# Time mixing in five slots per pair of heads, with two inverses and two last parts at work at once

## The chip, the cores and the metric

The kernel runs on one core of one Trainium2 chip. Its time is the device time in microseconds from start to end of one execution; the kernel before takes 2623.82 us (median of three runs, 2618.25 to 2625.08). All data and products are float32. Large products are done in a faster form, float32r, with each operand split into a rounded part and the rest (H and L in the code); small products are plain float32, and each of these shows up as two instructions in the trace.

## The reference: what is computed

A trunk of two layers on 256 tokens with 2048 channels. Layer 0 does RWKV-7 time mixing, layer 1 banded attention on one shared key and value; each is followed by a squared-ReLU MLP, and every part is scaled and shifted by vectors that are projected from a condition vector `c` (the "ada" products). The change touches time mixing only. With 32 heads of 64 channels it is

```
r, k, v = xr @ w_r, xk @ w_k, xv @ w_v
kk = normalised per head (k * k_k);  k = k * (1 + (a - 1) * k_a)
for t in range(256):                      # per head, S is 64 x 64
    sa = S @ (-kk_t)
    S  = S * w_t + outer(sa, kk_t * a_t) + outer(v_t, k_t)
    y_t = S @ r_t
y = group_norm(y) + (sum over the head of r * k * r_k) * v
out = (y * g) @ w_o
```

## The kernel before

**The chunked form.** The recurrence over 256 tokens is cut into four chunks of 64. Inside a chunk it becomes products of 64x64 matrices and the inverse of one unit triangular 64x64 matrix per chunk and head. Two heads share the 128 partitions, so the loop runs over 16 pairs of heads. Each pair passes through four stages, written as Python generators that give up control (`yield`) after each step:

- The dense stage, `proj_steps`: the two projections k and r of the pair, 2 x 16 steps. A step is one product with 512 columns (line 418) and one with 256 (line 419). It also loads the next weights (512 KB each, ring of six buffers `raw`) and splits them into H on ScalarE (line 384) and L on VectorE (line 387).
- `early`, 9 steps: decay, normalisation and the scaled factors `kr` and `bkh`, the centred values `G`, and the product of the bonus term. VectorE, ScalarE and GpSimd do most of it.
- `invert`, 11 steps: `both(pg, kr)` (line 105) makes the chunk's matrices, a masked copy of which is `X` (line 233). The inverse is then built by doubling from blocks of 2 to blocks of 64: levels 1 to 4 have a first step (`tiles`, line 112, then an addition on VectorE, line 253) and a second (`tiles`, then a transposed copy on VectorE, line 238, and a plain copy on ScalarE, line 269). The last level (lines 255 to 273) has two steps, read out by ScalarE. All results of this chain stand in one buffer of PSUM, `iv`.
- `late`, 10 steps: the chain over the four chunks. For each chunk it makes the right-hand side with the state `zs` (lines 294 and 297), copies it to `G` (299), then the next state (314, 317 or 319) and the outputs `py` (302, 322); behind it group norm, the bonus and the gate (330 to 339).

**The order of the work.** A period of the loop (lines 856 to 883) has in flight `late` of pair p-3, `invert` of p-2, `early` of p-1 and the dense stage of p. It has 11 slots; in each slot every generator advances by its share of steps, first the small ones, then the dense one. From this program order a planner fixes the order on each engine by a model of the durations: an instruction that is ready sooner may go ahead of an older one. `tc.issue_after` puts instructions behind a given one on their engine; here it holds the dense steps behind the small products of the slot before. The small products are not held. The program adds the waits between engines. After 16 pairs come three more periods that drain the pipeline; parts of the next product (`w_o`, `out_steps`, 44 steps) fill them, and `out_proj` does the rest.

**Other work in the loop.** In periods from 2 on, `ada` loads 512 KB of another weight per step into the same ring `raw` and adds it up on VectorE (line 448), five per period, 27 in the drain. Each half of such a vector ends in 32 small products (`ada_sum`, line 460), spread over slots by `fin(2)`.

Of the kernel before, what the change touches and what calls it, by code (L numbers as in the profile page):

```python
# [2 lines left out]

# [14 lines left out]
P = 128  # L18
# [58 lines left out]
class Pair:  # L77
# [3 lines left out]
    EARLY = 9  # L81
# [16 lines left out]
    def both(self, o, rhs):  # L98

        for c in range(4):  # L100
            for half in range(2):
                for i, K, S in self.heads:
                    n = i ^ half
                    nc = self.b.nc
                    nc.tensor.matmul(o[i][C * n:C * n + C, c, :], self.bkh[K, c, i + n, :], rhs[K, c, :],  # L105
                                     start=True, stop=True, tile_position=(C * i, C * n))

    def tiles(self, o, lhsT, rhs, pairs):

        for c in range(4):  # L110
            for R, K in pairs:
                self.b.nc.tensor.matmul(o[QS[K], c, :], lhsT[QS[R], c, :], rhs[QS[R], c, :], start=True, stop=True,  # L112
# [14 lines left out]
    def head_sums(self, ps, parts):  # L127
        for i, t in enumerate(parts):
            self.b.nc.tensor.matmul(ps, self.b.bones, t, start=(i == 0), stop=(i == 1))

    def early(self):
        b, nc, j, k, r, v, s, ch = self.b, self.b.nc, self.j, self.k, self.r, self.v, self.s, self.ch
        pw, vec, cst, e01 = b.pw, b.vec, b.cst, self.e01
        lw = pw.tile([96, 2, P], F32, tag="lw", bufs=2, name="lw")
        nc.sync.dma_start(out=lw, in_=b.d["lora2"][j, :96, 0:2])
        self.lg = pw.tile([P, 2, P], F32, tag="lg", bufs=2, name="lg")
        nc.sync.dma_start(out=self.lg, in_=b.d["lora2"][j, :, 2:4])
        z = b.psm()
        nc.tensor.matmul(z[:, 0:T], lw[:, 0, :], self.tw, start=True, stop=True)
        nc.tensor.matmul(z[:, T:2 * T], lw[:, 1, :], self.ta, start=True, stop=True)  # L140
# [8 lines left out]
        for o in (sw, a):  # L149
# [12 lines left out]
        self.pc = pw.tile([P, 4, 1], F32, tag="pc", bufs=3, name="pc")  # L162
# [11 lines left out]
        self.dg = pw.tile([P, 4, C], F32, tag="dg", bufs=1, name="dg")  # L174
        nc.gpsimd.tensor_tensor(out=self.dg, in0=cst("eye").unsqueeze(1).to_broadcast([P, 4, C]),
                                in1=self.pc.to_broadcast([P, 4, C]), op=ALU.mult)
# [7 lines left out]
        kr = self.kr = self.big("kr", 3)  # L184
        nc.vector.tensor_tensor(out=kr[:, :, 0:C], in0=ch(kk), in1=e0, op=ALU.mult)
        bkh = self.bkh = pw.tile([P, 4, 3, C], F32, tag="bkh", bufs=1, name="bkh")
# [3 lines left out]
        rkp = s()  # L190
        nc.vector.scalar_tensor_tensor(out=rkp, in0=r, scalar=vec("r_k", j), in1=km, op0=ALU.mult, op1=ALU.mult)
        nc.vector.tensor_tensor(out=bkh[:, :, 0, :], in0=ch(km), in1=ch(e2), op=ALU.mult)
        nc.scalar.copy(bkh[C:P, :, 2, :], bkh[C:P, :, 0, :])
        rkp = self.parts(AF.Copy, rkp)
        yield


        G = self.G = pw.tile([P, 2, 4, C], F32, tag="G", bufs=2, name="G")
        pt = b.psm().rearrange("p (a c k) -> p a c k", a=2, c=4)[:, 0]
        for c in range(4):  # L200
            for i, K, S in self.heads:
                nc.tensor.matmul(pt[K, c, :], ch(v)[K, c, :], cst("cen")[K], start=True, stop=True)
        for i, K, S in self.heads:
            nc.scalar.copy(G[K, i], pt[K])
        yield
        pbn = b.psm()[:, :T]
        self.head_sums(pbn, rkp)
        nc.vector.tensor_tensor(out=v, in0=pbn, in1=v, op=ALU.mult)
        yield

    def invert(self):
        b, nc, s, ch, kr = self.b, self.b.nc, self.s, self.ch, self.kr
        cst, pp = b.cst, b.pp

        def every(name):
            return cst(name).unsqueeze(1).to_broadcast([P, 4, H])

        def half(name, bufs):
            return b.pw.tile([P, 4, H], F32, tag=name, bufs=bufs, name=name)


        ui = cst("ui").unsqueeze(1).to_broadcast([P, 4, P])
        X = self.X = b.pw.tile([P, 2, 4, 3, C], F32, tag="X", bufs=2, name="X")
        pg = [pp.tile([P, 4, P], F32, tag="gr", bufs=1, name="gr"),
              pp.tile([P, 16, H], F32, tag="iv", bufs=1, name="iv").rearrange("p (c a) h -> p c (a h)", c=4)]
        self.both(pg, kr)
# [975 lines left out]
```

## Time and profile before

| | before |
|---|---|
| median of three runs | 2623.82 us |
| the profiled execution | 2621.53 us, span 2619.7 us, granted clock 0.994 |
| TensorE busy (products) | 2572.8 us, 98% |
| VectorE / ScalarE / GpSimd busy | 76% / 55% / 8% |
| pair loop: first `r` complete to last `r` complete | 198.4 to 584.5 us |
| drain of the pairs | 584.5 to 661 us |

PE is TensorE, PEld its weight loads, which overlap its products and show the order and pace of its instructions; DVE is VectorE, ACT ScalarE, POOL GpSimd. Busy time of PE is that of pipelined products with modelled ends, so in stretches of small products the starts of the weight loads tell more than the busy share. A mark such as [0.25 <-ACT u L269] on a row is the idle time of the engine before it and what ended it. Line numbers are those of the kernel before.

### The profile page before, as it was taken

How to read it: one execution, taken by the hardware profiler on the slowest of the kernel's cores; microseconds unless marked ns; L12 is line 12 of the kernel's file. 1: busy time of each engine (PE TensorE's matmuls, PEld its weight loads, DVE VectorE, ACT ScalarE, POOL GpSimd, SP SyncE). 2: the span in 40 equal slices, each digit the busy share in tenths (PEclk: the TensorE clock that was granted, in tenths of full speed). 3: DMA queues.
4: the chain of work that ended last, by engine and by line, in shares of the span. 5: the costliest groups of instructions: out<-in, count | busy, mean ns of one | idle time of the engine just before them, and what ended most of it. 6: DMA issues, size and time to landing. Idle time of an engine off the chain costs nothing.

```text
span 2619.7 us, 59049 instructions
## 1 busy us (share of the span) xinstructions
PE 2572.8 (98%) x24138; PEld 2232.6 (85%) x24138; DVE 1988.8 (76%) x2756; ACT 1452.8 (55%) x2709; POOL 207.2 (8%) x366
## 2 busy tenths in 40 slices
PE   7999999999999999999999999999999999999998
PEld 6997777778898888888888998778998888888887
DVE  5678888888778988888888887776779655555554
ACT  3456767674575633466544664676566533566443
POOL 0004333332100000000000000000000000000010
PEclk9999999999999999999999999999999999999999
DMA  9965666557858999999989788866559655555553
GB/s 360 356 239 184 190 189 193 186 181 255 288 182 304 344 367 360 353 332 335 330 313 330 260 302 286 277 233 207 183 193 338 227 188 187 191 186 188 190 188 125
DMA packets 192671, 662.74 MB, mean 253 GB/s; under 512 B 21392, under 2 KB 36112, under 8 KB 192400
## 3 DMA queue, kind: packets, MB, share of 16 engines
q1 hardware_dynamic: 191536, 657.71, 72.3%
q8 instruction: 189, 3.10, 0.5%
q10 hardware_dynamic: 864, 1.26, 0.1%
q14 instruction: 82, 0.67, 0.1%
HBM read 656.79 MB, written 2.10 MB: 252 GB/s over the span
## 4 chain that ended last, share of the span: by engine, by line
PE 90%; DVE 4%; DMA 3%; ACT 2%; issue 1%; POOL 1%; SPq 0%; DVEq 0%; ACTq 0%; POOLq 0%
PE pj L418 44%; PE pj L419 22%; PE pj L408 2%; PE pj L409 2%; PE pj L407 2%; PE iv L112 2%; DVE wL L387 1%; PE m L664 1%; DMA rawa<-w_ada 1%; DMA rawt<-w_ada 1%; PE gr L105 1%; POOL s L171 1%; PE v L767 1%; PE l L757 1%; PE po L1101 1%
## 5 line engine op out<-in xcount | busy, mean ns | idle before, releaser
L418 PE MATMUL pj<-aHL,wH 128*128 128x512 f32 x4128 | 1486.4, 401 | 0.0
L387 DVE TENSOR_TENSOR wL<-raw,wH 128x1024 fp32r<-128x1024 f32 x772 | 936.0, 1218 | 348.8 <-ACT wH L384 344.2
L384 ACT CAST wH<-raw 128x1024 fp32r<-128x1024 f32 x772 | 802.6, 1044 | 684.5 <-PE pj L418 567.0
L419 PE MATMUL pj<-aHL,wL 128*128 128x256 f32 x4128 | 1161.3, 281 | 1.2 <-DVE wL L387 1.1
L418 PEld LDWEIGHTS pj<-aHL,wH 128*128 128x128 f32 x4128 | 779.0, 189 | 185.2 <-issue 7.2
L419 PEld LDWEIGHTS pj<-aHL,wL 128*128 128x128 f32 x4128 | 780.4, 189 | 7.1 <-DVE wL L387 4.9
L418 PE MATMUL pj<-hHL,wH 128*128 128x512 f32 x992 | 348.1, 395 | 0.0
L448 DVE SCALAR_TENSOR_TENSOR acc<-rawm,ct,acc 128x1024 f32<-128x1024 f32 x217 | 279.9, 1290 | 2.6 <-DMA rawm<-w_ada 0.3
L419 PE MATMUL pj<-hHL,wL 128*128 128x256 f32 x992 | 275.5, 278 | 0.0
L418 PEld LDWEIGHTS pj<-hHL,wH 128*128 128x128 f32 x992 | 186.1, 188 | 43.2
L419 PEld LDWEIGHTS pj<-hHL,wL 128*128 128x128 f32 x992 | 186.4, 188 | 0.0
L409 PE MATMUL pj<-aHL,wL 128*128 128x258 f32 (+1 forms) x608 | 171.3, 282 | 1.6 <-DVE wL L387 1.6
L408 PE MATMUL pj<-aHL,wH 128*128 128x258 f32 (+1 forms) x608 | 172.6, 284 | 0.0
L407 PE MATMUL pj<-aHL,wH 128*128 128x258 f32 (+1 forms) x608 | 172.1, 283 | 0.0
L515 POOL TENSOR_TENSOR ss<-ss,scr 128x256 f32<-128x256 f32 x42 | 38.7, 922 | 1586.5 <-ACT scr L511 1586.3
L448 DVE SCALAR_TENSOR_TENSOR acc<-raw,ct,acc 128x1024 f32<-128x1024 f32 x90 | 120.2, 1336 | 0.1
L409 PEld LDWEIGHTS pj<-aHL,wL 128*128 128x128 f32 x608 | 116.0, 191 | 2.2 <-DVE wL L387 2.2
L408 PEld LDWEIGHTS pj<-aHL,wH 128*128 128x128 f32 x608 | 115.0, 189 | 0.1
L407 PEld LDWEIGHTS pj<-aHL,wH 128*128 128x128 f32 x608 | 114.4, 188 | 0.2
L984 DVE SCALAR_TENSOR_TENSOR x<-pj,mod,x 128x256 f32<-128x256 f32 x126 | 60.8, 483 | 55.7 <-PE pj L419 47.1
L948 ACT ACTIVATE t<-t 128x256 f32<-128x256 f32 x104 | 43.4, 418 | 89.7 <-DVE t L947 89.7
L448 DVE SCALAR_TENSOR_TENSOR acc<-rawt,ct,acc 128x1024 f32<-128x1024 f32 x53 | 67.8, 1280 | 16.2 <-DMA rawt<-w_ada 15.9
(268 smaller groups left out, 2981.6 us busy)
## 6 DMA issues: line engine op xcount, KB each, us to landing
raw<-w_up SPq DMA_DIRECT2D x256, 512.0 KB, 4.9
raw<-w_down SPq DMA_DIRECT2D x256, 512.0 KB, 4.6
rawm<-w_ada SPq DMA_DIRECT2D x166, 512.0 KB, 7.0
raw<-w_ada SPq DMA_DIRECT2D x97, 512.0 KB, 3.7
rawa<-w_ada SPq DMA_DIRECT2D x64, 512.0 KB, 8.1
rawm<-w_ada_kv SPq DMA_DIRECT2D x64, 512.0 KB, 6.6
rawt<-w_ada SPq DMA_DIRECT2D x57, 512.0 KB, 6.2
raw<-w_k SPq DMA_DIRECT2D x32, 512.0 KB, 4.2
```

Source lines behind the costliest of these rows:

```text
L112: self.b.nc.tensor.matmul(o[QS[K], c, :], lhsT[QS[R], c, :], rhs[QS[R], c, :], start=True, stop=True, tile_position=(H * R, H * K))
L384: nc.scalar.copy(Hf, raw)
L387: eng.tensor_tensor(out=Lf, in0=raw, in1=Hf, op=ALU.subtract)
L407: nc.tensor.matmul(ps, H[:, i, :], a(kt)[:, 0, :], start=(first and kt == 0), stop=False)
L408: nc.tensor.matmul(ps, H[:, i, :], a(kt)[:, 1, :], start=False, stop=False)
L409: ins = nc.tensor.matmul(ps, L[:, i, :], a(kt)[:, 0, :], start=False, stop=(last and kt == KT - 1))
L418: nc.tensor.matmul(ps, H[:, i, :], a(kt), start=(first and kt == 0), stop=False)
L419: ins = nc.tensor.matmul(ps[:, 0, :], L[:, i, :], a(kt)[:, 0, :], start=False, stop=(last and kt == KT - 1))
L448: nc.vector.scalar_tensor_tensor(out=acc, in0=raw, scalar=ck, in1=acc, op0=ALU.mult, op1=ALU.add)
L515: (eng or nc.gpsimd).tensor_tensor(out=self.ss, in0=self.ss, in1=sq, op=ALU.add)
L948: nc.scalar.activation(t, t, AF.Relu)
L984: nc.vector.scalar_tensor_tensor(out=x, in0=ps[:, i, :], scalar=self.mods[(layer, 5)][:, n:n + 1], in1=x, op0=ALU.mult, op1=ALU.add)
```

## The change

Seven things are changed together, all in time mixing and its drain.

1. Slots per period go from 11 to 5. `invert` (now 10 steps) and `late` (10 steps) each last two periods, so that in each slot the pipeline holds two inverses and two last parts, five generators in all with `early` (8 steps). There are 21 periods instead of 19. `ORDER` fixes which generator goes first in a slot: the older inverse, the younger one, then the others.
2. Every small product of the loop is put behind the TensorE instruction before it (`mm`, with `pinned`), and the dense steps behind the last small product: TensorE's order is the program order.
3. The matrix to be inverted comes from 16 products of its own at the end of `early` (`pd`, then one copy `near`). `both(pg, kr)`, `X`, `G` and `both(pt, dg)` move from `early` and `invert` to `late`.
4. The chain over chunks: the right-hand sides without state are made for all four chunks at once (`pa`), `M` (for the inner two chunks the matrix that takes a state to the next) is made ahead with the help of `kT`, then `state` makes three states `Z`, one per step, and one step each makes all right-hand sides and all outputs.
5. The buffers in PSUM: `iv` becomes one tile of four blocks that are used in turn, `chn` one tile of two blocks; `py` also holds the bonus product.
6. The ring `raw` falls from 6 to 3 buffers in the loop. Outside of it every second load goes to a second ring of 3 (`wx`). More buffers for `kr`, `bkh`, `u` and others.
7. The sums of the ada vectors are done in one go at slot 3 (`fin(HK)`). In the drain 40 steps of `w_o` run instead of 44; the rest follows in `out_proj`. Weights are split at steps 5 and 11 instead of 6 and 15.

```diff
-    EARLY = 9
+    EARLY, INV, LATE = 8, 10, 10
...
+        pd = self.chain()
         for c in range(4):
+            for q in range(4):
+                i = 1 - q // 2
+                K, h = self.heads[i][1], H * (q % 2)
+                b.mm(pd[QS[q], c, :], bkh[K, c, 1, h:h + H], kr[K, c, h:h + C], start=True, stop=True,
+                                 tile_position=(C * i, H * q))
+        near = pw.tile([P, 4, C], F32, tag="da", bufs=2, name="da")
+        nc.scalar.copy(near, pd)
+        da, u = near[:, :, 0:H], self.half("u", 5)
...
     def invert(self):
...
-            pi = pp.tile([P, 16, H], F32, tag="iv", bufs=1, name="iv")[:, 0:4, :]
+            pi = self.block()
...
     def late(self):
...
+        pg = [self.wide(), b.psm().rearrange("p (c k) -> p c k", c=4)]
+        self.both(pg, kr)
...
+        bn = self.parts(AF.Copy, self.rkp)
+        yield
+        pa = self.chain()
+        for c in range(4):
+            for i, K, S in heads:
+                b.mm(pa[S, c, :], X[K, i, c, 0, :], G[K, i, c, :], start=True, stop=True)
+        for i, K, S in heads:
+            nc.scalar.copy(G[S, i], pa[S])
+        pt = self.pair_of_banks()
+        self.both(pt, dg)
+        for c in (1, 2):
+            for i, K, S in heads:
+                b.mm(pt[i][S, 3 + c, :], kr[K, c, 0:C], cst("eye")[K], start=True, stop=True)
...
+        yield
+        pr = self.pair_of_banks()
+        for n in range(4):
+            for m in range(2):
+                for i, K, S in heads:
+                    O = S if m == 0 else K
+                    b.mm(pr[m][O, n, :], u[S, n, :], X[S, i, n, 1 + m, :], start=True, stop=True,
+                                     tile_position=(S.start, O.start))
...
+        def state(c, ps):
+            if c:
+                for i, K, S in heads:
+                    b.mm(ps[K, 0, :], M[K, c - 1, :], Z[K, c - 1, :], start=True, stop=False)
+            for i, K, S in heads:
+                b.mm(ps[K, 0, :], X[:, i, c, 2, :], G[:, i, c, :], start=c == 0, stop=True)
+            nc.scalar.copy(Z[:, c, :], ps[:, 0, :])
+
+        ps = self.chain()
+        for c in (1, 2):
+            for i, K, S in heads:
+                b.mm(ps[K, c, :], kT[S, c - 1, :], X[S, i, c, 2, :], start=True, stop=True)
+        state(0, ps)
+        nc.vector.tensor_tensor(out=M, in0=ps[:, 1:3, :], in1=dg[:, 1:3, :], op=ALU.add)
+        yield
+        state(1, self.chain())
+        yield
+        state(2, self.chain())
+        yield
+        pa = self.chain()
+        for c in (1, 2, 3):
+            for i, K, S in heads:
+                b.mm(pa[S, c, :], X[K, i, c, 0, :], G[K, i, c, :], start=c == 1, stop=False)
+        for c in (1, 2, 3):
+            for i, K, S in heads:
+                b.mm(pa[S, c, :], kr[K, c, 0:C], Z[K, c - 1, :], start=False, stop=c == 3)
+        for i, K, S in heads:
+            nc.scalar.copy(G[S, i, 1:4], pa[S, 1:4])
+        yield
...
-    RAW_BUFS = 6
+    RAW_BUFS = 3
...
-    SLOTS = 11
+    SLOTS = 5
+    _INV = (("invert", 1), ("invert", 0))
+    ORDER = ((*_INV, ("late", 1), ("late", 0), ("early", 0)),) * 3 + ((*_INV, ("early", 0), ("late", 0), ("late", 1)),) * 2
+    DRAIN_STEPS = (10, 7, 7, 8, 8)
...
+    def raw_ring(self):
+        self.nraw += 1
+        if self.wx is not None and self.nraw % 2:
+            return self.wx, "rawx", self.RAW_BUFS
+        return self.wp, "raw", self.RAW_BUFS
...
+    def mm(self, *args, **kw):
+        with self.tc.issue_after(self.last_pe()) if self.pinned else nullcontext():
+            self.nc.tensor.matmul(*args, **kw)
...
+            iv = pi.tile([P, 4, 4, C // 2], F32, name="iv")
+            chn = pp.tile([P, 2, 4, C], F32, name="chn")
+            self.blocks = cycle(iv[:, i] for i in range(4))
+            self.chains = cycle(chn[:, i] for i in range(2))
...
-                        if kt in (6, 15) and src is not None:
+                        if kt in (5, 11) and src is not None:
...
-            stages = ((Pair.late, 10), (Pair.invert, 11), (Pair.early, Pair.EARLY), (None, 2 * KT))
+            stages = ((Pair.late, Pair.LATE, 2), (Pair.invert, Pair.INV, 2), (Pair.early, Pair.EARLY, 1),
+                      (None, 2 * KT, 1))
...
+                    order = sorted(live, key=lambda g: self.ORDER[slot].index(g[3]))
+                    for gens in (order, [dense]):
+                        with nullcontext() if gens is order else tc.issue_after(self.last_pe()):
+                            for g in gens:
                                 while g[2] * self.SLOTS < g[1] * (slot + 1):
                                     next(g[0], None)
                                     g[2] += 1
```

More of the change, by code (lines that the diff above doesn't have):

```diff
@@ L2 @@
 from contextlib import ExitStack, nullcontext
+from itertools import cycle
 import numpy as np
@@ L128, in head_sums @@
         for i, t in enumerate(parts):
[L129 removed]
+            self.b.mm(ps, self.b.bones, t, start=(i == 0), stop=(i == 1))
     def early(self):
@@ L211, in invert @@
-    def invert(self):
[L212 to L226, printed above, removed]
-        da, u = half("da", 2), half("u", 3)
-        for i, K in enumerate(QS):
-            n = H * (i % 2)
-            nc.scalar.copy(da[K], pg[1 - i // 2][K, :, n:n + H])
-        nc.gpsimd.tensor_tensor(out=u, in0=da, in1=every("lev0"), op=ALU.mult)
-        for i in (1, 0):
-            nc.vector.tensor_tensor(out=X[:, i, :, 0:2, :].rearrange("p c a t -> p c (a t)"), in0=pg[i], in1=ui,
-                                    op=ALU.mult)
-        def turned(src):
-            t = half("tt", 1)
-            nc.vector.transpose(out=t.rearrange("p c t -> p (c t)"), in_=src.rearrange("p c t -> p (c t)"))
-            return t
-        nc.vector.tensor_tensor(out=u, in0=u, in1=every("eye_h"), op=ALU.add)
-        tt_ = turned(u)
-        yield
@@ new lines, in early, with half, every, turned @@
+        nc.gpsimd.tensor_tensor(out=u, in0=da, in1=self.every("lev0"), op=ALU.mult)
+        nc.vector.tensor_tensor(out=u, in0=u, in1=self.every("eye_h"), op=ALU.add)
+        self.tt = self.turned(u)
+        yield
+    def half(self, name, bufs):
+        return self.b.pw.tile([P, 4, H], F32, tag=name, bufs=bufs, name=name)
+    def every(self, name):
+        return self.b.cst(name).unsqueeze(1).to_broadcast([P, 4, H])
+    def turned(self, src):
+        t = self.half("tt", 2)
+        self.b.nc.vector.transpose(out=t.rearrange("p c t -> p (c t)"), in_=src.rearrange("p c t -> p (c t)"))
+        return t
@@ new lines, in wide, with block, chain, pair_of_banks @@
+    def wide(self):
+        return self.b.pp.tile([P, 4, P], F32, tag="gr", bufs=1, name="gr")
+    def block(self):
+        return next(self.b.blocks)
+    def chain(self):
+        return next(self.b.chains)
+    def pair_of_banks(self):
+        return [t.rearrange("p c k -> p (c k)").rearrange("p (e k) -> p e k", k=C)
+                for t in (self.wide(), self.b.psm().rearrange("p (c k) -> p c k", c=4))]
+    def invert(self):
+        b, nc = self.b, self.b.nc
+        half, every = self.half, self.every
+        da, u, tt_, turned = self.da, self.u, self.tt, self.turned
@@ new lines, in late @@
+        pg = [self.wide(), b.psm().rearrange("p (c k) -> p c k", c=4)]
+        self.both(pg, kr)
+        for i in range(2):
+            nc.vector.tensor_tensor(out=X[:, i, :, 0:2, :].rearrange("p c a t -> p c (a t)"), in0=pg[i], in1=ui,
+                                    op=ALU.mult)
+        G = pw.tile([P, 2, 4, C], F32, tag="G", bufs=2, name="G")
+        pt = self.chain()
+        for c in range(4):
+            for i, K, S in heads:
+                b.mm(pt[K, c, :], ch(v)[K, c, :], cst("cen")[K], start=True, stop=True)
@@ new lines, in late @@
+        for i, K, S in heads:
+            nc.scalar.copy(G[K, i], pt[K])
+        dg = pw.tile([P, 4, C], F32, tag="dg", bufs=1, name="dg")
+        nc.gpsimd.tensor_tensor(out=dg, in0=cst("eye").unsqueeze(1).to_broadcast([P, 4, C]),
+                                in1=pc.to_broadcast([P, 4, C]), op=ALU.mult)
+        bn = self.parts(AF.Copy, self.rkp)
+        yield
+        pa = self.chain()
+        for c in range(4):
+            for i, K, S in heads:
+                b.mm(pa[S, c, :], X[K, i, c, 0, :], G[K, i, c, :], start=True, stop=True)
```

186 lines of the change are left out of this document (83 added, 103 removed).

## The prediction, on record before the result

> **What bounds the kernel now.** I read the page first (busy shares, then the chain), then busy time by windows over the pair loop, then one pair in order of time.
>
> ```profile
> PE 2572.8 (98%) x24138; PEld 2232.6 (85%) x24138; DVE 1988.8 (76%) x2756; ACT 1452.8 (55%) x2709; POOL 207.2 (8%) x366
> ...
> PE 90%; DVE 4%; DMA 3%; ACT 2%; issue 1%; POOL 1%; SPq 0%; DVEq 0%; ACTq 0%; POOLq 0%
> ```
>
> TensorE carries the end: 90% of the chain. The windows (us, then busy time of PE, PEld, DVE, ACT, POOL, granted clock, DMA share, GB/s) show where the change lies.
>
> ```profile
> 238.50:584.50 346.00, 341.74 (x7145) 272.56 (x7146) 301.15 (x571) 247.19 (x689) 117.95 (x195) 1.00 0.59 187
> 584.50:661.00 76.50, 70.96 (x1315) 60.41 (x1305) 67.46 (x105) 38.08 (x104) 15.49 (x23) 0.96 0.75 244
> ...
> 433.00:459.50 26.50, 26.20 (x533) 20.90 (x533) 23.39 (x45) 18.95 (x54) 9.15 (x16) 1.00 0.61 191
> ```
>
> The 13 periods from 238.5 to 584.5 take 26.6 us each, the drain behind them 76.5. TensorE idles about 0.3 us in a period, VectorE is next with 23.4 of 26.5. So a period is the sum of what TensorE is given, as long as nothing makes it wait. One slot and its neighbours, by weight loads (PEld: TensorE's own sequence) and by the readers of its results:
>
> ```profile
> 434.34 0.34 PEld L112 LDWEIGHTS iv<-tt,al 32*32 32x32 f32 x32
> 434.72 0.19 PEld L418 LDWEIGHTS pj<-aHL,wH 128*128 128x128 f32 x1
> 435.02 0.28 DVE L253 TENSOR_TENSOR xs<-iv,csts 128x128 f32<-128x128 f32 x1
> 435.07 0.19 PEld L418 LDWEIGHTS pj<-aHL,wH 128*128 128x128 f32 x1
> 435.54 0.19 PEld L419 LDWEIGHTS pj<-aHL,wL 128*128 128x128 f32 x1
> 435.98 0.14 PEld L294 LDWEIGHTS chn<-G,X 64*64 64x64 f32 x2 [0.25 <-issue]
> 436.09 0.20 PEld L297 LDWEIGHTS chn<-zs,kr 64*64 64x64 f32 x4
> 436.35 0.34 PEld L112 LDWEIGHTS iv<-u,xs 32*32 32x32 f32 x32
> 436.74 0.19 PEld L418 LDWEIGHTS pj<-aHL,wH 128*128 128x128 f32 x1
> 437.93 0.30 DVE L238 STREAM_TRANSPOSE tt<-iv 128x128 f32<-128x128 f32 x1
> 438.27 0.27 ACT L269 COPY u<-iv 128x128 f32<-128x128 f32 x1 [1.37 <-DVE tt L238]
> 438.65 0.39 PEld L112 LDWEIGHTS iv<-tt,al 32*32 32x32 f32 x32 [0.34 <-issue]
> 439.08 0.19 PEld L418 LDWEIGHTS pj<-aHL,wH 128*128 128x128 f32 x1
> 439.73 0.28 DVE L253 TENSOR_TENSOR xs<-iv,csts 128x128 f32<-128x128 f32 x1
> 440.70 0.34 PEld L112 LDWEIGHTS iv<-u,xs 32*32 32x32 f32 x32
> 441.09 0.19 PEld L418 LDWEIGHTS pj<-aHL,wH 128*128 128x128 f32 x1
> 441.79 0.27 ACT L269 COPY u<-iv 128x128 f32<-128x128 f32 x1 [0.39 <-DVE tt L238]
> 445.13 0.54 PEld L202 LDWEIGHTS ms<-csts,v 64*64 64x64 f32 x14
> 445.73 0.19 PEld L418 LDWEIGHTS pj<-aHL,wH 128*128 128x128 f32 x1
> 446.97 0.33 PEld L257 LDWEIGHTS iv<-tt,X 32*32 32x32 f32 x16 [0.24 <-issue]
> 447.34 0.19 PEld L129 LDWEIGHTS ms<-sH,bones 128*128 128x128 f32 x1
> 447.46 0.55 ACT L261 ACTIVATE xs<-iv 32x128 f32<-32x128 f32 x2 [0.29 <-PE iv L257]
> ```
>
> A dense step (L418 and L419) takes 435.07 - 434.72 = 0.35 us, so 32 of them 11.2. From the last L419 to the next small product is 0.44 where 0.23 is usual: 0.21 is lost at each turn from dense to small. L297's four loads take 0.26 until the 32x32 products begin where 0.05 to 0.1 would do: another 0.16 to 0.2 for that turn. Leaving 32x32 products costs 0.05 (0.39 from start to next against 0.34).
>
> **The products, before and after.** Small products per pair, in instructions (one fp32 product is two): before 466 (the window's 533 less 64 dense, to the nearest boundary). After, counted from the diff: first part 38 (the 32 of `pd` new), inverse 288 as before, last part 224, together 550. The inverse loses its 32 of `both(pg, kr)` and 32 of `both(pt, dg)`, which move to the last part, and reads its strips from `pd`; new are `kT` (8), the state matrices (8), and the chain's products X·G once more over all chunks.
>
> Prices. L112: 0.34 for 32. The 64x64 products with 64 columns on two tiles of the array: L202, 14 in 0.60, so 0.04 each. On all four tiles they are cheaper:
>
> ```profile
> 458.14 0.13 PEld L105 LDWEIGHTS gr<-dg,bkh 64*64 64x64 f32 x1
> ...
> 458.56 0.14 PEld L105 LDWEIGHTS ms<-dg,bkh 64*64 64x64 f32 x1
> ...
> 451.99 0.69 PEld L307 LDWEIGHTS ms<-X,uf 64*64 64x64 f32 x12
> ```
>
> 32 take 0.42 there, 0.013 each. Groups that stand in both kernels drop out: z, `pg` (L337), three head sums, `both` twice, centring, L314 and L322 (as many products in the state and `py` steps). What differs, before to after: L307 0.91 (16 at 0.057) to `pr` on four tiles 0.42; L294, L297 and L302, interleaved, 0.74 (three times 435.98 to 436.35 less the turn, 0.21, and half of that for the first chunk) to `pa` early 16 x 0.04 = 0.6, `pa` late 24 x 0.04 = 0.9, Z·kr 12 x 0.04 = 0.5 and M·Z 8 x 0.04 = 0.3; new `pd` 0.42, `kT` 0.3, `M` 0.3. The sum is -0.5 + 1.6 + 1.0, about **+2.1 us per pair**, for 16 pairs +34.
>
> Against it stand the turns. From 11 slots to 5 saves 6 x 0.21 = 1.3 per pair. Eight of the ten inverse steps were entered from other small products (0.16 each, 1.3); now the older one is entered from the dense part, whose turn is counted, and the younger from the older at nothing; five exits fewer save 0.25. The last part, cut finer and mixing 128x64 with 64x64 products, adds some 7 turns (1.1). That is **-1.7 us per pair**, -27. The whole loop's slots, 19 x 11 against 21 x 5, fall a little less than 6 per pair: +2. Without waits the change is worth about +9 us.
>
> The Trainium skill (TensorEngine Tiling (Array Packing), Instruction Overhead) says that a product with one column takes as long as one with 60. By that rule all small products would cost alike, the 84 more per pair at 0.34/32 would be 0.9 and not 2.1 us, and the sum would be 1.2 x 16 = 19 us lower; the rows 0.34 (32 columns) and 0.42 (64 columns) for 32 products bear it out only in part.
>
> **The waits.** Here I expect the loss. Before, each inverse step is followed by dense work while VectorE and ScalarE empty its result. After, the four blocks of the inverses are slices of one PSUM tile (`iv`, 2,048 bytes a partition), and the order is written out: older inverse's products, younger inverse's products, the rest. Do slices of one tile wait for each other's readers? Two rows of before say yes:
>
> ```profile
> 655.75 0.47 ACT L332 ACTIVATE sl<-py,csts 128x256 f32<-128x256 f32 x1 [4.79 <-PE py L129]
> 656.71 0.48 DVE L334 SCALAR_TENSOR_TENSOR sl<-py,vecs,sl 128x256 f32<-128x256 f32 x1 [1.50 <-ACT sl L333]
> 657.25 0.70 PE L337 MATMUL py<-tg,lg 128*128 128x256 f32 x2 [1.53 <-DVE sl L334]
> ```
>
> L337 writes the second half of `py`; L334 reads the first half and gives L337 nothing. The last reader of the second half, L332, ended at 656.22, yet TensorE idles 1.53 us until L334 ends at 657.19. Likewise L269, above, waits 1.37 for L238, though both only read `iv`. So the younger inverse will wait in every slot until the older one's result is read out, with nothing put between.
>
> The Trainium skill (PSUM — Partial Sum Buffer, PSUM bank collisions raise a hardware error) says why: two engines may not touch one bank and quadrant at a time, reads included, and software has to order them. By that rule the blocks can't go free of these waits, which speaks for the forecast and against the first rival below.
>
> The price, from the moment TensorE could go on to the end of the last reader, plus 0.12 until TensorE starts (L337 starts 0.06 after its wait ends; the products at 438.65 0.11 after L269's 438.54). A step of the second kind (transpose, then copy): 438.54 - 436.74 + 0.12 = 1.92 and 442.06 - 441.09 + 0.12 = 1.09, mean 1.5. A step of the first kind (L253): 435.30 - 434.72 + 0.12 = 0.70 and 440.01 - 439.08 + 0.12 = 1.05, mean 0.88. The last level (two copies): 448.01 - 447.34 + 0.12 = 0.79. The older inverse has two of the second kind, one of the first, two of the last level: 5.5 us per period at these means. With the smaller of each two it is 2 x 1.09 + 0.70 + 2 x 0.79 = 4.5. Readers queue because VectorE is busy 23.4 of 26.5; with a longer period it has more room, so I take the 4.5. The lower bound is the readers alone with 0.12 on either side: 2 x (0.30 + 0.27 + 0.24) + (0.28 + 0.24) + 2 x (0.55 + 0.12) = 3.5. Both inverses share 15 periods: **+68 us** (52 to 83).
>
> `chn` becomes one tile with two blocks as well. Twice in a period its user changes with nothing between: slot 1, late `pa` of the older pair, two copies of 64x192, then `pa` of the younger; slot 4, `pd`, a copy of 128x256, then the state step. The nearest row:
>
> ```profile
> 440.96 0.44 ACT L299 COPY G<-chn 64x64 f32<-64x64 f32 x2
> ```
>
> It ends at 441.40, 0.70 after L297's products gave way to L112's at 440.70; with the longer copies 0.8 to 1.0, and 0.7. For 15 and 13 periods **+21 us** (0 if ScalarE is prompt and the gap hidden, to 28).
>
> **Hidden, and what if not.** ScalarE and VectorE trade work nearly even: -0.54 of L319 against one add for `M`; four copies of strips, eight of `G`, one of `bkh` against one of `near`, four of `G`, two of `kT`, two more of X, two of Z. All lies under TensorE's period. `lg` is loaded two slots ahead of use. The ring of raw weights falls from 6 to 3 buffers in the loop:
>
> ```profile
> raw<-w_r SPq DMA_DIRECT2D x6, 512.0 KB, 4.2
> ```
>
> That is the landing in the loop (406 to 486 us). In the drain (585 to 660), and what follows a landing:
>
> ```profile
> raw<-w_ada SPq DMA_DIRECT2D x24, 512.0 KB, 5.4
> raw<-w_o SPq DMA_DIRECT2D x9, 512.0 KB, 5.5
> ```
>
> ```profile
> L387 DVE TENSOR_TENSOR wL<-raw,wH 128x1024 fp32r<-128x1024 f32 x772 | 936.0, 1218 | 348.8 <-ACT wH L384 344.2
> L384 ACT CAST wH<-raw 128x1024 fp32r<-128x1024 f32 x772 | 802.6, 1044 | 684.5 <-PE pj L418 567.0
> ```
>
> In the loop 9 loads in 26.5 us leave each buffer 8.8 us for a landing of 4.2 and cast and subtraction of 2.3: hidden. In the drain 33 loads in 76.5 us leave 7.0 against 5.4 + 2.3 = 7.7; in a drain of 100 us they are hidden again, in one of 76 they cost 33 x 0.7 / 3 = 8. I take 0 (0 to +20). The output products moved behind the drain (two of sixteen chunks for four blocks) cost the same there as here. The bursts of the sums at slot 3 save part of 1 us in every third period: within the turns.
>
> **The sum.** 2621.5 (profiled execution; span 2619.7; 2 us under the median 2623.8) + 34 - 27 + 2 + 68 + 21 = 2719.5; I say **2720**. Own range: with 52, 0 and 10 less for the products 2621.5 + 9 + 52 - 10 = 2673; with 83, 28, the ring's 20 and 5 for turns 2621.5 + 9 + 83 + 28 + 25 = 2767.
>
> **Rivals.** *First, the other side: the blocks go free of each other.* Place: `iv` and `chn`, every slot. Then the 89 us of waits vanish and products against turns decide: +9 us, less the 0.3 that TensorE idles in a period and the 5.5 in the drain (10), less 16 if a two-tile product costs nearer 0.03: 2605 to 2630, say 2615, not slower. It decides as soon as a slot's waits cost under 0.1 us. For it: only one tile of before shows a product held by a reader of another slice. Against it: the 1.53 us there. *Second, the ring of three binds in the loop too*: slower VectorE readers behind a late load, one landing beyond its 8.8 us a period by 2 us, 16 x 2 on top of 2720: 2752. For it: landings of 5.5 in the drain; against: 0.61 DMA share in the loop.
>
> **How the numbers follow.** Forecast 0.71, first rival 0.23, second 0.06. Faster or slower begins at 0.3%, 8 us, about what a measurement tells from no change. The first rival gives 0.15 faster and 0.08 same; the others, 0.77, are slower. The forecast's own range is 2673 to 2767; for 8 in 10 the range reaches into the first rival: **2608 to 2767**.
>
> **What would show it.** Right: periods of 32 to 34 us between two `k` evacuations; TensorE idle before the younger inverse's L-lines of `iv`, put down to the copy of `u`, the transpose or `xs`; VectorE's share of a period down to about 70%. The product part: 13 to 16 us of small products and turns per period with these idles taken off. Wrong: periods under 27 us, or idle time before `iv` under 0.3 us a slot; then the first rival holds. Idle at L418 on the cast or subtraction would be the second.

## The result and the profile after

The changed kernel takes 2743.69 us (median, 2740.86 to 2745.97) against 2622.62 us before on the same chip: 1.0463 times as long, 95% interval 1.0444 to 1.0482. The forecast was 2720 with a range of 2608 to 2767. The profiled executions span 2743.4 and 2619.7 us, so there are 123.7 us to account for.

The page of the changed kernel, busy time and chain:

```profile
PE 2605.8 (95%) x25482; PEld 2276.2 (83%) x25482; DVE 1997.0 (73%) x2740; ACT 1457.5 (53%) x2677; POOL 191.6 (7%) x366
...
PE 68%; DVE 2%; ACT 2%; DMA 1%; issue 1%; DVEq 0%; SPq 0%; POOL 0%; ACTq 0%; POOLq 0%
```

TensorE is busy 2605.8 us and idle 2743.4 - 2605.8 = 137.6. Before it was busy 2572.8 and idle 46.9. So of the 123.7 us, **90.7 are idle time of TensorE and 33.0 are busy time**. No other engine became the bound: VectorE's and ScalarE's busy times moved by less than 9 us.

Where it lies is shown by windows from the first evacuation of `r` to the fifth (the fill), to the sixteenth (eleven whole periods), and to the last write of `v` (the drain). Columns: length, then busy time and instructions of PE, PEld, DVE, ACT and POOL, granted clock, DMA share, GB/s. The kernel before:

```profile
198.44:291.95 93.51, 90.16 (x1624) 72.10 (x1624) 79.53 (x143) 63.56 (x165) 34.47 (x51) 0.98 0.58 185
291.95:584.49 292.54, 288.86 (x6074) 230.26 (x6067) 254.78 (x485) 209.60 (x585) 99.83 (x165) 1.00 0.59 186
584.49:660.00 75.51, 69.97 (x1308) 59.54 (x1300) 66.61 (x103) 37.52 (x102) 15.49 (x23) 0.95 0.75 246
```

The changed kernel, the same three stretches, then four single periods:

```profile
202.87:291.60 88.73, 72.32 (x1319) 59.32 (x1317) 74.06 (x124) 49.75 (x116) 34.13 (x46) 0.94 0.59 188
291.60:660.24 368.64, 307.58 (x6990) 256.71 (x6994) 259.79 (x476) 210.51 (x561) 83.92 (x165) 0.96 0.47 149
660.24:778.60 118.36, 96.12 (x2008) 83.93 (x2006) 72.54 (x114) 53.88 (x144) 16.65 (x28) 0.87 0.53 166
...
464.40:496.70 32.30, 26.84 (x614) 22.36 (x614) 23.74 (x42) 19.07 (x52) 7.57 (x15) 1.00 0.49 154
394.80:432.30 37.50, 31.79 (x678) 26.40 (x678) 22.87 (x43) 19.02 (x51) 7.60 (x15) 0.86 0.43 131
432.30:464.40 32.10, 26.60 (x614) 22.23 (x614) 23.64 (x42) 18.97 (x51) 7.55 (x15) 1.00 0.47 149
595.50:627.60 32.10, 27.09 (x678) 22.82 (x678) 22.27 (x42) 19.02 (x52) 7.50 (x15) 1.00 0.47 155
```

The eleven periods take 76.1 us more (33.5 each in place of 26.6), the drain 42.9 more, the fill 4.8 less. What is left, 9.5, lies ahead of the fill (4.4) and behind the drain (5.1). TensorE's idle time (length less its busy time) grew by 61.1 - 3.7 = 57.4 us in the eleven periods, 16.7 in the drain and 13.1 in the fill.

One period in order of time, by weight loads, with one step's two readers (478.77 and 479.11). It begins at 464.40; L531 issues every small product:

```profile
465.05 0.37 PEld L531 LDWEIGHTS iv<-tt,al 32*32 32x32 f32 x32 [1.25 <-issue]
471.88 0.34 PEld L531 LDWEIGHTS iv<-u,xs 32*32 32x32 f32 x32 [0.53 <-DVE xs L242]
473.91 0.43 PEld L531 LDWEIGHTS chn<-G,X 64*64 64x64 f32 x12 [0.88 <-ACT G L349]
478.00 0.34 PEld L531 LDWEIGHTS iv<-u,xs 32*32 32x32 f32 x32 [0.25 <-DVE acc L491]
478.77 0.30 DVE L213 STREAM_TRANSPOSE tt<-iv 128x128 f32<-128x128 f32 x1
479.11 0.27 ACT L258 COPY u<-iv 128x128 f32<-128x128 f32 x1 [0.43 <-DVE tt L213]
479.49 0.37 PEld L531 LDWEIGHTS iv<-tt,al 32*32 32x32 f32 x32 [1.14 <-issue]
485.76 0.34 PEld L531 LDWEIGHTS iv<-u,xs 32*32 32x32 f32 x32 [0.75 <-ACT xs L250]
490.44 0.37 PEld L531 LDWEIGHTS iv<-tt,al 32*32 32x32 f32 x32 [0.80 <-issue]
492.04 0.20 PEld L531 LDWEIGHTS chn<-Z,M 64*64 64x64 f32 x4 [0.70 <-ACT da L197]
```

At 478.00 the older inverse multiplies. Its result is transposed (478.77) and copied (479.11, done at 479.38), and only then, at 479.49, the younger inverse starts, in another block of the same tile. That happens five times in the period, with idle times of 1.25, 0.53, 1.14, 0.75 and 0.80 us. The two rows of `chn` show the same between two chains (0.88) and between `pd` and the state step (0.70). Together 6.1 us; TensorE's own idle in this period is 32.30 - 26.84 = 5.5, where it was 0.3 in a period before. The loads marked `issue` name no releaser, but the products they load for do: the copy of `u` at 465.08 and 479.52, that of `uf` at 490.47. Counted by the products in place of their loads, the same seven waits are 4.0 us (`iv`) and 1.3 (`chn`), 5.3 of the 5.5.

The same by releaser, over 300 to 600 us (nine periods; us in total, times, longest):

```profile
PE iv L531 <- ACT u L258: 20.5, 18, 1.4
...
PEld iv L531 <- ACT xs L250: 8.0, 9, 1.0
PEld chn L531 <- ACT G L349: 7.9, 9, 0.9
...
PE iv L531 <- ACT uf L262: 6.5, 9, 0.8
```

### The profile page after: what moved, and what is told of

It reads as the page before. It is cut to its first block, busy times and chain, and to the rows that moved or that the text cites. A ratio compares the mean times of both kernels' runs of the same rounds, so it can differ in the third digit from the quotient of the medians.

```text
span 2743.4 us, 61680 instructions
## 1 busy us (share of the span) xinstructions
PE 2605.8 (95%) x25482; PEld 2276.2 (83%) x25482; DVE 1997.0 (73%) x2740; ACT 1457.5 (53%) x2677; POOL 191.6 (7%) x366
## 4 chain that ended last, share of the span: by engine, by line
PE 68%; DVE 2%; ACT 2%; DMA 1%; issue 1%; DVEq 0%; SPq 0%; POOL 0%; ACTq 0%; POOLq 0%
PE pj L461 38%; PE pj L462 19%; PE pj L451 2%; PE pj L452 2%; PE pj L450 2%; DVE wL L429 1%; DMA raw<-w_o 1%; PE po L1171 1%; DMA rawt<-w_ada 0%; PE py L531 0%; ACT wH L426 0%; PE o L452 0%; PE o L450 0%; PE m L531 0%; DVE acc L491 0%
## 5 line engine op out<-in xcount | busy, mean ns | idle before, releaser
L426 ACT CAST wH<-raw 128x1024 fp32r<-128x1024 f32 x424 | 443.4, 1046 | 452.8 <-PE pj L461 376.2
L429 DVE TENSOR_TENSOR wL<-raw,wH 128x1024 fp32r<-128x1024 f32 x424 | 517.4, 1220 | 137.4 <-ACT wH L426 134.9
L429 DVE TENSOR_TENSOR wL<-rawx,wH 128x1024 fp32r<-128x1024 f32 x348 | 424.0, 1218 | 227.0 <-ACT wH L426 225.5
L426 ACT CAST wH<-rawx 128x1024 fp32r<-128x1024 f32 x348 | 363.5, 1044 | 278.9 <-PE pj L461 223.5
```

The costliest lines, as they stand in the source:

```text
L426: nc.scalar.copy(Hf, raw)
L429: eng.tensor_tensor(out=Lf, in0=raw, in1=Hf, op=ALU.subtract)
```

## The experiments

The theory (**W**): the products wait for the readers of their own PSUM tile, whichever block of it they use, and the written order puts nothing in between. The rivals: **P**, the products and their turns are simply dearer and the waits cover nothing that counts; **O**, the fixed order of the products costs by itself; **R**, the ring of three raw buffers costs.

**Two tiles in place of one** (`e1_banks`). The pair's parity chooses the tile; an inverse and the chain of the same pair share it.

```diff
-        return next(self.b.blocks)
+        return self.b.blocks[self.j % 2]
...
-        return next(self.b.chains)
+        return self.b.chains[1 if self.j >= NPAIR - 2 else self.j % 2]
...
-            iv = pi.tile([P, 4, 4, C // 2], F32, name="iv")
-            chn = pp.tile([P, 2, 4, C], F32, name="chn")
...
+            banks = [pi.tile([P, 512], F32, name="iv0"), pp.tile([P, 512], F32, name="iv1")]
...
```

> Two PSUM tiles in place of iv and chn, each with a block for an inverse and one for the chain; pairs of even number use the one, of odd number the other. Products and their order are those of the changed kernel; only the place of their results differs. Theory W (the loss is the younger inverse waiting for the readers of the older one's result in the same tile, 4.7 us a period between 464 and 497 us, and the same at chn, 1.7): the waits between the inverses go, and some come back where the chain now follows an inverse in its own tile (about 3 us a period by the same readers), so 3 to 4 us less in each of 15 periods: 2680 to 2700. Rival P (the added products, the turns and the fixed order cost the time, the waits only fill slack): no change, 2735 to 2750.

Measured: 2722.35 us, 1.0381 times the kernel before (1.0364 to 1.0397). That lies between the two expectations. The trace says why: the inverses no longer wait for each other (the younger one's load at 447.62 follows the older one's at 447.37 with no idle time), but the chain that follows an inverse in its own tile now waits, and the 2.81 us at 437.40 are longer than any wait they replaced:

```profile
437.40 0.51 PEld L531 LDWEIGHTS iv<-X,kT 64*64 64x64 f32 x8 [2.81 <-ACT u L258]
...
447.37 0.34 PEld L531 LDWEIGHTS iv<-u,xs 32*32 32x32 f32 x32 [0.25 <-issue]
447.62 0.40 PEld L531 LDWEIGHTS iv<-tt,al 32*32 32x32 f32 x32
448.97 0.19 PEld L531 LDWEIGHTS iv<-Z,M 64*64 64x64 f32 x4 [0.95 <-ACT u L258]
```

The wait moved with the tile, as W has it. I had priced this new neighbour too low, at some 3 us a period in all: the products held by the copy of `u` alone wait 31.3 us from 300 to 600 us, where the changed kernel has 20.5.

**Other work between the two inverses** (`e2_order`). Tiles as changed, the order in a slot rewritten.

```diff
-    ORDER = ((*_INV, ("late", 1), ("late", 0), ("early", 0)),) * 3 + ...
+    ORDER = ((("late", 1), ("invert", 1), ("late", 0), ("invert", 0), ("early", 0)),) * 3 + (
+        (("early", 0), ("invert", 1), ("late", 0), ("invert", 0), ("late", 1)),) * 2
```

> The changed kernel with another order in a slot: older last part, older inverse, younger last part, younger inverse, first part (slots 0 to 2), first part, older inverse, younger last part, younger inverse, older last part (slots 3 and 4). One tile for all inverses as in the changed kernel. W: other products now lie between two users of a tile, some 2 of 6.4 us of waits are left, some 5 turns more at 0.2 are paid: 3 to 4 us a period less, 2680 to 2700. P: turns are added and nothing is saved: 2755 to 2765.

Measured: 2679.87 us, 1.0218 (1.0201 to 1.0235), 64 us less than the changed kernel, with the same products in the same tiles. P falls with this alone: the products are the same, and only what stands between them changed. Of the 66.2 us between the spans 46.9 are idle time of TensorE and 19.3 busy time, at a clock of 0.992 against 0.983. The eleven periods take 29.0 us each; the longest wait left in a period is for `chn` (one of 0.99 before a product of `iv` is put down to `sL` on GpSimd):

```profile
439.43 0.43 PEld L532 LDWEIGHTS chn<-G,X 64*64 64x64 f32 x12 [1.00 <-ACT G L349]
```

**One block in place of four** (`e3_one_block`). Both inverses write the same quarter of `iv`.

```diff
-            self.blocks = cycle(iv[:, i] for i in range(4))
+            self.blocks = cycle(iv[:, 0] for i in range(4))
```

> The changed kernel with one block of iv for all inverses instead of four used in turn. W (waits go by the tile, not by the slice): the same time as the changed kernel within 0.3%, 2735 to 2752. Rival S (waits go by slices, so the four blocks do help): the younger inverse now waits where it did not, and the time rises by 30 us or more.

Measured: 2739.94 us, 1.0450 (1.0428 to 1.0471): as the changed kernel, whose interval it overlaps. In the waits (300 to 600 us) the largest releaser has the very figures of the kernel with four blocks:

```profile
PE iv L531 <- ACT u L258: 20.5, 18, 1.4
```

So four blocks in one tile buy no independence at all.

**The order left free** (`e4_free`). Tiles and program as changed, but the planner may move small products past each other.

```diff
-            going, self.pinned = {}, True
+            going, self.pinned = {}, False
```

> The changed kernel with the small products no longer put behind the TensorE instruction before them; the planner orders them by its own model. W: the planner can put other ready products of the slot between the two inverses, the waits shrink, 2660 to 2720. Rival O (the order is not what costs): 2735 to 2750.

Measured: 2678.29 us, 1.0215 (1.0197 to 1.0232). The planner finds the cover that the written order lacks: the waits for the copy of `u` fall from 20.5 us to

```profile
PE iv L531 <- ACT u L258: 0.5, 2, 0.3
```

TensorE idles 69.7 us in place of 137.6. Its busy time stays at 2604.5 us, though the clock is 0.992; `e2_order` is busy 2586.5 at the same clock, so the order of the products changes their busy time too.

**Two tiles, and the chain in the other one** (`e6_apart`, with the two tiles of `e1_banks`): a pair's chain goes where its inverse is not, and last parts stand between the inverses in four of five slots.

```diff
-        return next(self.b.chains)
+        return self.b.chains[1 if self.j >= NPAIR - 2 else 1 - self.j % 2]
...
-    ORDER = ((*_INV, ("late", 1), ("late", 0), ("early", 0)),) * 3 + ...
+    ORDER = ((("invert", 1), ("late", 1), ("late", 0), ("invert", 0), ("early", 0)),) * 3 + (
+        (*_INV, ("late", 1), ("late", 0), ("early", 0)),
+        (("early", 0), ("invert", 1), ("late", 1), ("late", 0), ("invert", 0)))
```

> The changed kernel with its small products in two PSUM tiles by the parity of the pair, the chain of a pair in the tile that the inverse of that pair does not use, and in the first four slots of a period one of the last parts written between the two inverses. Theory W (the loss of the loop is waits of a product for the readers of the same PSUM tile): the two inverses no longer share a tile and no chain stands directly behind an inverse of its own tile, so that some 0.4 us of the 6.4 us of waits per period are left: a period of 26.5 to 27.5 us, the whole 2640 to 2665, with the longer drain still in it. Rival P (the products themselves and their turns are dearer than before, the waits are hidden anyway): a period above 29 us, the whole above 2690.

Measured: 2662.98 us, 1.0157 (1.0139 to 1.0174), within W's 2640 to 2665, 81 us under the changed kernel; its page, and its fill, eleven periods and drain:

```profile
PE 2584.3 (97%) x25482; PEld 2254.6 (85%) x25482; DVE 1996.7 (75%) x2740; ACT 1453.1 (55%) x2677; POOL 200.0 (8%) x366
```

```profile
201.22:283.19 81.97, 68.97 (x1300) 56.57 (x1302) 71.26 (x123) 48.45 (x115) 35.89 (x46) 0.98 0.62 196
283.19:590.12 306.93, 297.75 (x7022) 246.61 (x7023) 259.96 (x474) 209.26 (x560) 91.21 (x165) 0.99 0.57 179
590.12:696.65 106.53, 89.98 (x2008) 76.71 (x2007) 74.59 (x116) 52.19 (x144) 15.91 (x28) 0.95 0.59 187
```

The idle time in the eleven periods is 9.2 us where the changed kernel has 61.1; a period is 27.9, somewhat above the 26.5 to 27.5 that I expected. Two readings matter below. TensorE is busy 2584.3 us with the same 25,482 products that took the changed kernel 2605.8. And the drain still takes 31 us more than before. The largest single idle time left is again a product held by a reader of another half of its tile (`py`), 1.5 us where I had expected 0.4 of all waits:

```profile
445.15 0.73 PEld L533 LDWEIGHTS py<-tg,lg 128*128 128x128 f32 x4 [1.51 <-DVE sl L368]
```

**The same with the order left free** (`e7_apart_free`: the edits of `e6_apart` and of `e4_free`).

> The kernel with two tiles and the chain apart, and the planner free to move small products past each other in place of the fixed product order. Theory W: with the waits gone already the free order has little to hide: within 10 us of the kernel with the chain apart, 2635 to 2665. Rival O (the fixed order costs time of its own, apart from the waits, for example in the drain): 20 us or more under it, below 2630.

Measured: 2661.33 us, 1.0155 (1.0139 to 1.0170), no different. The fixed order costs 65 us in the changed kernel, where all inverses share a tile, and nothing that shows in `e6_apart`, where consecutive users have different tiles: O falls as a cause of its own.

**The ring alone, in the kernel before** (`e8_before_ring3`).

```diff
-    RAW_BUFS = 6
+    RAW_BUFS = 3
...
+    def raw_ring(self):
+        self.nraw += 1
+        if self.wx is not None and self.nraw % 2:
+            return self.wx, "rawx", self.RAW_BUFS
+        return self.wp, "raw", self.RAW_BUFS
...
```

> The kernel before with one part of the change alone: the ring of raw weights at three buffers in the loop, as the changed kernel has it. Theory of the prediction (9 loads in 26.6 us leave each of three buffers 8.8 us, a landing takes 4.2 and its cast and subtraction 2.3): no change in the loop, 0 to 8 us in the drain, 2622 to 2631. Rival (the ring binds in the loop): one landing per period late by 2 us, 2650 or more.

Measured: 2645.36 us, 1.0088 (1.0075 to 1.0101): 24 us, three times the upper end of my expectation, though under the rival's. Eleven periods take 294.7 us against 292.5, so the loop is not bound. The spans differ by 24.9: 7.4 come up to the fifth evacuation, 4.1 in the drain and 11.3 behind it, where output weights land late. Only 15.1 of them are idle time of TensorE; 9.8 are the same 24,138 products taking longer (2582.6 us against 2572.8, with a granted clock of 0.990 against 0.994). From the drain on (594 to 780 us), the kernel with three buffers:

```profile
ACT wH L390 <- DMA raw<-w_o: 15.2, 10, 4.8
...
PE o L414 <- ACT wH L390: 6.7, 5, 3.6
```

The kernel before, 584 to 760 us:

```profile
ACT wH L384 <- DMA raw<-w_o: 6.4, 7, 1.5
```

**The fixed order alone, in the kernel before** (`e9_before_pinned`): every small product behind the one before it in the program, through a helper, and the dense steps behind the latest small product.

```diff
...
+    def mm(self, *args, **kw):
+        with self.tc.issue_after(self.last_pe()) if self.pinned else nullcontext():
+            self.nc.tensor.matmul(*args, **kw)
```

> The kernel before with one part of the change alone: the order of the products on TensorE fixed as in the changed kernel (small products in the order of the program, dense work behind the latest small product). Theory W: its program puts dense work between dependent products already, so that the fixed order has little to wait for: 2620 to 2645. Rival O (the fixed order by itself costs what the free order of the changed kernel won back, 65 us): 2670 or more.

Measured: 2630.17 us, 1.0029 (1.0018 to 1.0041), as W has it: some 8 us.

**The fifth slot in another order** (`e11_order4`, on `e6_apart`), so that the gate product of the row above comes last.

```diff
-        (("early", 0), ("invert", 1), ("late", 1), ("late", 0), ("invert", 0)))
+        (("early", 0), *_INV, ("late", 0), ("late", 1)))
```

> The kernel with the chain apart, its fifth slot in another order: both inverses and the younger last part ahead of the older last part, whose gate product (it writes the second half of the tile whose first half VectorE still reads) then comes last in the slot. Theory W: that product waited 1.5 us behind the reader of the other half and will wait no more, the two steps that move together wait some 0.4: 1.1 us less per period, the whole 2640 to 2652. Rival (the wait was hidden behind TensorE's queue, or moves to the next product): within 5 us of the kernel with the chain apart, 2658 to 2668.

Measured: 2665.13 us, 1.0156 (1.0140 to 1.0172): a miss for W, no different from `e6_apart`, as the rival has it. The wait is gone in the trace,

```profile
421.62 0.37 PEld L533 LDWEIGHTS iv<-tt,al 32*32 32x32 f32 x32 [0.35 <-issue]
...
422.64 0.73 PEld L533 LDWEIGHTS py<-tg,lg 128*128 128x128 f32 x4
```

but the last seven of the eleven periods take 27.6 us against 28.0, a third of what I took for it, and the first evacuation of `r` comes 2.9 us later (204.1 against 201.2). TensorE idles 2.3 us less and is busy 5.2 longer, at a clock of 0.990 against 0.993. Why, I did not settle.

**A fourth raw buffer** (`e12_ring4`, on `e11_order4`; room from one buffer less each for `kr`, `rkp` and `s`).

```diff
+        if self.pinned and self.nraw % 4 == 0:
+            return self.pw, "rawy", 1
```

> The same kernel with a fourth buffer in the ring of raw weights while the pair loop runs (room for it comes from one buffer less for kr, rkp and s each). Theory R (the ring of three costs the changed kernel in its drain what it cost the kernel before, 24 us): a third of the loss of depth is given back and more than half of the time, 10 to 20 us under the kernel with the other order of the fifth slot. Rival (the longer drain hides the landings, and its length is latency of the last pairs): within 5 us of it.

Measured: 2659.73 us, 1.0139 (1.0126 to 1.0153). 5 us under `e11_order4`, and the intervals overlap: R's 10 to 20 us did not come, and the rival's figure fits about. Its eleven periods are 27.2 us each, 7.6 us less in all than in `e11_order4`, but they begin 4.5 later,

```profile
290.31:589.88 299.57, 293.57 (x6983) 245.82 (x6985) 254.33 (x475) 208.77 (x560) 95.68 (x165) 1.00 0.58 183
589.88:695.66 105.78, 90.64 (x2004) 78.92 (x2004) 74.51 (x116) 53.00 (x144) 18.20 (x28) 0.94 0.60 189
```

and the drain is only 1.7 us shorter than with three. More than four buffers beside the changed kernel's tiles were not tried.

**One product of the change alone, in the kernel before** (`e10_before_pr4`): `pr` on four array tiles, in two banks, copied out in four pieces.

```diff
-                pr = b.psm().rearrange("p (c k) -> p c k", c=4)
+                pr = [b.psm()[:, 0:T].rearrange("p (c k) -> p c k", c=4) for _ in range(2)]
...
+                    for m in range(2):
+                        for i, K, S in heads:
+                            O = S if m == 0 else K
+                            nc.tensor.matmul(pr[m][O, n, :], u[S, n, :], X[S, i, n, 1 + m, :], ...
```

> The kernel before with one part of the change alone: the product that closes the last part (u with X, two blocks) on all four tiles of the array and in two banks, copied out in four pieces in place of two. By the rows of before and after it takes 0.42 in place of 0.91 us: some 0.3 to 0.45 us per pair, 5 to 7 us for 16 pairs, 2614 to 2618. Rival (the product is fed no faster or the four copies on ScalarE hold the next product): 2620 to 2626.

Measured: 2635.46 us, 1.0051 (1.0039 to 1.0064), 13 us slower and outside both expectations. The product did get cheaper (TensorE is busy 2565.2 us in place of 2572.8), but TensorE idles 20.2 us more. The second bank is the one that the next pair's first product wanted:

```profile
407.45 0.30 PEld L139 LDWEIGHTS ms<-tw,lw 96*128 96x128 f32 x2 [1.69 <-ACT X L313]
```

**The same with its first half in `py`** (`e13_before_pr4_py`).

```diff
+                pr = [t.rearrange("p (c k) -> p c k", c=4) for t in (py, b.psm()[:, 0:T])]
```

> The kernel before with the closing product of the last part on four tiles of the array as in the last experiment, but its first half in the free half of py instead of a second ms bank. In the last experiment the first products of the next pair (z, in ms) waited 1.4 us per period for the copies that empty the second ms bank. Theory: the product itself is about 0.5 us per pair cheaper, and only the ms bank took that back: with ms as before, 0.5 x 16 = 8 us under the kernel before, 2611 to 2618, and no wait before z. Rival: the four copies in place of two hold the next product of the chain instead, 2622 or more.

Measured: 2620.67 us against 2621.81, ratio 1.000 (0.999 to 1.0009): no change, between the two expectations. The wait at L139 is gone, and the chain's next products now come in three pieces behind the copies, with dense steps and their turns in between:

```profile
455.15 0.19 PEld L317 LDWEIGHTS chn<-G,X 128*64 128x64 f32 x2 [0.35 <-ACT X L313]
...
455.55 0.19 PEld L317 LDWEIGHTS chn<-G,X 128*64 128x64 f32 x2 [0.21 <-ACT X L313]
...
455.95 0.20 PEld L325 LDWEIGHTS py<-X,G 128*64 128x64 f32 x4 [0.21 <-ACT X L313]
```

TensorE is busy 4.1 us less than before and idle 2.3 more: the waits for the copies take back much of what the product saves, and what is left is within the noise. No kernel tried beats the one before.

## Why the prediction was right, and where it was not

**The waits were the loss, and their price held.** "So the younger inverse will wait in every slot until the older one's result is read out": the five rows of `iv` above sum to 4.5 us per period, for which I had taken 4.5; the two of `chn` to 1.58, where I had 1.6 (by the products, 4.0 and 1.3). Covering them by order (`e2_order`), by the planner (`e4_free`) or by tiles (`e6_apart`) gives back 64, 65 and 81 us. With 89 us forecast, TensorE's idle time grew by 90.7. That the two are so near is in part luck, for the place was only partly right: my price of 89 for 15 periods makes 65 in eleven, where 57.4 were found, and 24 elsewhere, where 29.8 lie in the fill and the drain alone. There, part is not the waits I priced, for `e6_apart`, with those gone, still idles 13.0 and 16.6 us there against 3.4 and 5.5 before.

The Trainium skill (PSUM — Partial Sum Buffer, PSUM bank collisions raise a hardware error), as quoted in the prediction, has software order two engines in one bank. The runs agree in this much: within one tile nothing went free (`e3_one_block`), in separate tiles the inverses did (`e1_banks`). Whether it is the bank or the tile that decides, no run here tells apart.

**Products, turns and slots: +9 us held as a sum.** One term of it has the wrong sign: 19 x 11 - 21 x 5 = 104 slots are 6.5 per pair, more than the 6 counted, so that the +2 should have been about -2 and the sum +5. `e6_apart` has the changed kernel's products without most of its waits, though in another order, at nearly the clock of before (0.993 against 0.994): busy 2584.3 - 2572.8 = 11.5 us more. The Trainium skill (TensorEngine Tiling (Array Packing), Instruction Overhead) would have made the sum 19 us lower, 10 us less than before; the trace does not bear that out. Of the single terms only `pr` was run alone: 0.91 to 0.42 us makes 7.8 us for 16 pairs, and TensorE's busy time fell by 7.6 (`e10_before_pr4`) and 4.1 (`e13_before_pr4_py`). The other terms were not, and neither run got faster for it.

**The term that was missing: the clock.** The sum came out 24 us short of the median, 25.7 short of the profiled span. Of these 1.7 are idle (90.7 against 89), 2.5 products (11.5 against 9), and 2605.8 - 2584.3 = 21.5 are the same 25,482 products taking longer in the changed kernel than in `e6_apart`, with a granted clock of 0.983 against 0.993. My sum priced every product at the full clock of the rows before. The two kernels differ where the clock does. In the last seven of the eleven periods it is 0.99 in both, and TensorE is busy equally long (the changed kernel, then `e6_apart`):

```profile
432.30:660.24 227.94, 189.29 (x4406) 158.16 (x4410) 166.89 (x306) 134.60 (x361) 53.06 (x105) 0.99 0.48 151
394.33:590.12 195.79, 189.54 (x4438) 157.05 (x4440) 165.38 (x304) 134.00 (x360) 58.71 (x105) 0.99 0.56 178
```

In the first four the changed kernel is busy 118.29 us at 0.92, `e6_apart` 108.21 at 1.00, and 118.29 x 0.92 = 108.8. That the clock makes up the whole 21.5 is still inferred, not isolated by a run, and the order of the products counts as well: `e4_free` is busy 2604.5 us at 0.992.

**The drain was not costed.** I wrote of "a drain of 100 us" only to judge the ring. It takes 118.4 us against 75.5: five periods hang over where three did. Part is work moved there from the fill (TensorE busy 26.2 us more in the drain, 17.8 less in the fill), part idle time (16.7). With nearly all waits of the loop covered, 31 us stay (`e6_apart`), with a fourth buffer 30. It did not show in the total because I charged waits to 15 periods, and what four of them were charged came near what the fill and the drain idled for these other reasons too. How the rest splits into late weights and the length of the last pairs' own chain stays open.

**The ring.** "In the loop 9 loads in 26.5 us leave each buffer 8.8 us": right for the loop (2.2 us in eleven periods). "I take 0 (0 to +20)": in the kernel before it costs 24, outside my upper end, because I reckoned with evenly spaced loads and looked no further than the drain, while nearly half of it, 11.3 us, comes behind it. In the changed kernel its share is not measured: the fourth buffer's 5 us in all cannot be told from none, though it took 7.6 us off the eleven periods of one profiled run.

**The rivals.** The first, blocks free of each other, is refuted by the idle rows and by `e3_one_block`. The second, the ring binding in the loop, would be idle time of the dense steps on the cast or subtraction, which the changed kernel's waits do not show in the loop.

**What would show it:** periods of 32 to 34 us, found 32.1 to 34.7 (between evacuations of `r`) but for two of 35.8 and 37.5; idle before the younger inverse put down to `u`, the transpose or `xs`, found; VectorE near 70% of a period, found 23.74 / 32.30 = 73%; 13 to 16 us of small products and turns, found 26.84 - 11.2 = 15.6.

## What to carry to other kernels

When two chains are put side by side to cover each other, look first at where their results land: in one PSUM tile, each hand-over between them cost 0.5 to 1.3 us here, however the tile was cut into blocks, and three different covers won back 64 to 81 of the 121 us lost. Put consecutive users into different tiles, and check who follows them there, since in `e1_banks` and `e10_before_pr4` the wait just moved to the next user of the tile. Count fill and drain when a pipeline gets deeper, with the buffers that feed them; a ring that is ample in the steady loop (2.2 us) cost 23 us outside it. And when waits are added to a sum, expect more than the waits: here the clock fell in some of the stretches with idle time, and the products took longer there.

## What the hardware showed that I had not expected

The granted clock fell in some stretches where TensorE only paused briefly. Two periods shown above issue the same 678 loads: at clock 1.00 in 32.1 us with TensorE busy 27.1, at 0.86 in 37.5 us with TensorE busy 31.8. Slices of the slow period are lower still:

```profile
412.00:416.00 4.00, 3.58 (x92) 2.95 (x86) 1.94 (x4) 3.26 (x8) 0.95 (x1) 1.00 0.22 82
416.00:420.00 4.00, 3.35 (x65) 2.85 (x64) 1.99 (x6) 2.01 (x7) 0.61 (x1) 0.61 0.62 175
420.00:424.00 4.00, 3.79 (x27) 2.83 (x25) 3.23 (x4) 1.80 (x4) 0.73 (x1) 0.54 0.35 124
```

From 300 to 580 us TensorE idles 16% in the changed kernel and 13% in `e1_banks`, at clocks of 0.95 and 0.93; at 7% idle or less (`e2_order`, `e4_free`, `e6_apart`, `e12_ring4`) the clock is 0.99 to 1.00. The idle share alone does not decide: the changed kernel idles 16% in its first four full periods at 0.92 and 17% in the last seven at 0.99, and `e3_one_block`, with the same waits, 17% from 300 to 580 us at 0.99 and 16% from 580 to 661 at 0.90. What decides is open.

The Trainium skill (TensorE: Matmul & The Clock Gate, A second HAM failure mode: psum-queue depth-cycling) tells of such a case: small idle gaps between groups of products, where PSUM is cycled, make the gate swing. The rows agree in that the single waits in the changed kernel's loop are at most 1.6 us long and the clock falls all the same; that the cycling of PSUM is the reason, no run here shows.
